# v's weight sums moved behind k's head norm on GpSimd's queue, seven gate blocks in front, v's plain products first, and another order of the projections beside the pairs

## The chip, the cores and the metric

The kernel runs on one core of a Trainium2 chip. TensorE (PE) multiplies, VectorE (DVE) and ScalarE (ACT) work on tiles of up to 128 partitions in SBUF and PSUM, GpSimd (POOL) does small vector work and issues the accumulating transfers, SyncE (SP) issues most of the others. The metric is the device time of one execution in microseconds (us). Three runs of the kernel before took 416.15, 417.72 and 417.67 us, median 417.67. The trace comes from one more, profiled execution.

## The reference

One decoder layer on x (512 tokens by 1024 features, float32) with two attention branches of 8 heads of 64 each.

```python
h = rms_norm(x, norm_w)
qa, ka, va, za, qb, kb, vb, zb, gl_a, gl_b = split(h @ w_in)      # widths 512 x 8, then 1024 x 2
oa = moba(rms_norm(qa), rms_norm(ka), va, rel_bias)               # softmax branch "a", q and k normed by head
ob = stick_breaking(qb, kb, vb)                                   # branch "b": sigmoid and a running product
ya = (oa * silu(za)) @ w_up_moba
yb = (ob * silu(zb)) @ w_up_sb
y  = sigmoid(gl_a + gb_a) * ya + sigmoid(gl_b + gb_b) * yb
out = x + y @ w_out
```

## The kernel before

**Products.** Every float32 product is made of three matmuls in fp32r: each operand is split into a high part (an ACT copy into an fp32r tile, `wh` L163, `xh`) and a low part (a DVE subtraction, `wl` L165, `xl`), and `mm3` (L202 to L206) adds high x low, low x high and high x high. A weight block is 128 x 1024 (`wr`, 512 KB). `load_w` keeps three blocks ahead in the order of the list `stream`: SP loads, ACT makes `wh`, DVE makes `wl`. A block of a projection (`chunk_ct`) is 24 matmuls of 128x512.

**Stages.** First the q projection of branch a (`qa`, 96 matmuls), then k (`ka`, 96). Both get a norm by head: ACT squares (`kasq` L323), DVE reduces (L324), POOL makes the factor of each row in three small instructions for each of four row tiles (`kast` L325 to L327), DVE multiplies (`kan` L334), transposes (`kat` L353), and the result goes through DRAM (`kadr`) and comes back turned. Meanwhile PE does the first gate projections (`gl`, the list FRONT). In this stage DVE also makes the sums of x that the next stage needs (`mix_x`, L291 to L305: four half-width additions for each of four k, and two subtractions `ml`).

**v by seven products.** The two v projections (1024 columns together) are a 2 x 2 block product done with seven products instead of eight (Strassen's scheme in Winograd's form): sums `s1` to `s4` of x, and sums T1 to T4 of the weight blocks. `sum_v` (L108) makes a weight sum by DMA: it loads one block (L117, ACT's queue) and adds the other by an accumulating transfer from POOL's queue (L120). T2 is made of T1, and T4 of T2. `product` takes two weight blocks (24 matmuls) and adds up in two PSUM banks.

**Pairs.** Then come eight pairs of heads, four of branch a and four of branch b. For each: `scores` (12 pairs of matmuls), `softmax` or `stick` on DVE and ACT, `turn` (DVE transposes, L475), `put` (SP stores the weights of the head, L482) and `get` (ACT's queue loads them turned, L489: `pta` or `ptb`). `finish` of the pair before multiplies the weights with v (`poa`, `pob`, L501, 16 matmuls) and DVE multiplies by the silu gate (L505).

**What sets the order.** Beside each pair PE gets whole blocks of other projections, written out by hand in FILLS: four words for each pair (an empty word is no block), `za`/`zb` the silu gates, `q`/`k` the operands of branch b, `g` gates, `up` the two halves of a block of the up projection (each half one PSUM bank, evacuated by DVE, L617). These take turns in two PSUM banks ("pj"), which `finish` uses too. The row of a pair so holds three or four blocks. Instructions of an engine run in the order in which the program puts them on its queue; a scheduler has settled that order when the program is built.

Of the kernel before, what the change touches and what calls it, by code (L numbers as in the profile page):

```python
# [32 lines left out]
PQ = BLK[-1] * 32  # L33
# [9 lines left out]
Y_SUMS = {0: ("T2b",), 2: ("T3a", "T3b"), 5: ("T4a", "T4b")}  # L43


FRONT = ("g:0", "g:1", "g:2", "g:3", "g:4", "g:5")
FILLS = ("za:0", "za:1", "za:2", "",
         "za:3", "g:6", "g:7", "q:0",
         "k:0", "zb:0", "q:1", "",
         "k:1", "zb:1", "q:2", "k:2",  # L50
         "zb:2", "q:3", "k:3", "",
         "zb:3", "up:0", "g:8", "up:1",
         "g:9", "up:2", "g:10", "",
         "up:3", "g:11", "g:12", "",
         "g:13", "g:14", "g:15")


@with_exitstack
def hybrid_layer(ctx: ExitStack, tc: tile.TileContext, x, xT, w, rel, out):
    nc = tc.nc  # L60
    V, A, G, T = nc.vector, nc.scalar, nc.gpsimd, nc.tensor
# [37 lines left out]
    ahead, low, sums = [], {}, {}  # L99
    turn_of = cp.tile([1, 1], F32, name="turn_of")  # L100
    WO = w.shape[0] - len(BLOCKS)
    WV, VOUT = 8, [("v", name) for name in OUT]
    stream = list(range(WV)) + list(range(16, 16 + len(FRONT))) + VOUT + list(range(16 + len(FRONT), WO)) + OUT

    def block(name, base):
        return w[base + BLOCKS.index(name)]

    def sum_v(name, part):  # L108

        with tc.issue_after(last["qa"]):  # L110
            if name == "T4":
                sums["v", "T4" + part] = t = sums["v", "T2" + part]
            else:
                t = vp.tile([P, H // 2, 2, P], F32, tag="v", name=f"v{name}{part}").rearrange("p a b d -> p (a b d)")
                sums["v", name + part] = t
                with tc.issue_after(spread_r):
                    nc.scalar.dma_start(t, block(TERMS[name][0] + part, WV))  # L117
            two = TERMS[name][1] if name != "T4" else "21"
            src = sums["v", two + part] if two[0] == "T" else block(two + part, WV)
            nc.gpsimd.dma_start(t, src, accum_op=ALU.add)  # L120
# [161 lines left out]
    def normalize(k):  # L282

        raw = xraw[k]
        V.scalar_tensor_tensor(raw, raw, nw[:, k:k + 1], R, op0=ALU.mult, op1=ALU.mult)
        A.activation(xH[k], raw, AF.Copy)
        V.tensor_tensor(xL[k], raw, xH[k].bitcast(F32), op=ALU.subtract)
# [3 lines left out]
    def mix_x(k):  # L291

        a, b = xraw[k], xraw[k + 4]
        left, right = slice(0, HS), slice(HS, S)
        V.tensor_tensor(b[:, right], a[:, right], b[:, right], op=ALU.subtract)
        V.tensor_tensor(a[:, right], a[:, left], a[:, right], op=ALU.subtract)
        V.tensor_tensor(a[:, left], b[:, right], a[:, left], op=ALU.subtract)
        V.tensor_tensor(b[:, left], b[:, left], a[:, left], op=ALU.add)
        h = tp.tile([P, 4 * PQ], F32R, tag="pt", bufs=4, name=f"mx{k}")
        for n, raw in enumerate((a, b)):  # L300
            hi, lo = h[:, n * S:(n + 1) * S], slot(f"ml{k}{n}", F32R)
            A.activation(hi, raw, AF.Copy)
            V.tensor_tensor(lo, raw, hi.bitcast(F32), op=ALU.subtract)
            for cs, name in ((left, ("S2", "S4")[n]), (right, ("S3", "S1")[n])):
                mixed[name, k] = hi[:, cs], lo[:, cs]  # L305
# [94 lines left out]
    def bring(name):  # L400
        raws[name] = fetch(flipped[name], name)

    ps_ka = section_tc(1, "ka", hooks={0: lambda: norm(ps_qa, "qa", float(HD)),
                                       1: lambda: (normalize(0), normalize(1)),
                                       2: lambda: (normalize(2), normalize(3),
                                                   [sum_v(n, h) for n in ("T1", "T2", "T3") for h in "ab"]),
                                       3: lambda: (normalize(4), normalize(5), normalize(6), normalize(7),
                                                   spread(ps_qa, "qa"))})

# [119 lines left out]

    for i, word in enumerate(FRONT):  # L530
        f_g(int(word.split(":")[1]))
        if i == 0:
            norm(ps_ka, "ka", 1.0)
            bring("qa")
        elif i == 1:
            spread(ps_ka, "ka")
            mix_x(0)
        elif i == 2:
            qa.extend(split_flipped(raws["qa"], "qa"))
            mix_x(1)  # L540
        elif i == 3:
            bring("ka")
            mix_x(2)
        elif i == 4:
            mix_x(3)

    def product(ps, a, start):
# [8 lines left out]
    def values():  # L556

        v_of = {}
        for br in "ab":
            two = [vp.tile([P, H // 2, 2, P], F32, tag="v", name=f"v{br}s{t}").rearrange("p a b d -> p (a b d)")  # L560
                   for t in range(2)]
            v_of[br] = [two[t // 2][:, t % 2 * S:(t % 2 + 1) * S] for t in range(NT)]
        a11, a12 = ([(xH[k + d][:, :HS], xL[k + d][:, :HS]) for k in range(4)] for d in (0, 4))
        a22 = [(xH[k + 4][:, HS:], xL[k + 4][:, HS:]) for k in range(4)]
        s1, s2, s3, s4 = ([mixed[f"S{n}", k] for k in range(4)] for n in (1, 2, 3, 4))
        X, Z = ([bank("s", f"v{n}{t}") for t in range(2)] for n in "xz")
        product(X, a11, True)
        for t in range(2):
            A.activation(v_of["a"][t], X[t], AF.Copy)
        product(Z, a12, True)  # L570
        for t in range(2):
            V.tensor_tensor(v_of["a"][t], Z[t], v_of["a"][t], op=ALU.add)
        product(X, s2, False)
        for t in range(2):
            A.activation(v_of["b"][t], X[t], AF.Copy, scale=-1.0)
        ka.extend(split_flipped(raws["ka"], "ka"))
        Y = [bank("s", f"vy{t}") for t in range(2)]
        product(Y, s1, True)
        for t in range(2):
            A.activation(v_of["b"][2 + t], Y[t], AF.Copy)  # L580
        for h in "ab":
            sum_v("T4", h)
        product(X, s3, False)
        for t in range(2):
            V.tensor_tensor(v_of["b"][2 + t], v_of["b"][2 + t], X[t], op=ALU.subtract)
        product(Y, s4, False)
        for t in range(2):
            V.tensor_tensor(v_of["b"][t], Y[t], v_of["b"][t], op=ALU.add)
        product(X, a22, False)
        for t in range(2):  # L590
            A.activation(v_of["a"][2 + t], X[t], AF.Copy)
        return v_of
# [268 lines left out]
```

## Time and profile before

| | us |
|---|---|
| median of three runs (416.15, 417.72, 417.67) | 417.67 |
| the profiled execution | 416.63 |
| its span in the trace | 414.8 |
| PE busy | 390.6 |
| DVE busy | 287.6 |
| ACT busy | 208.3 |
| POOL busy | 68.1 |
| granted TensorE clock, mean over the span | 0.975 |

PE is busy 94% of the span, so the time is PE's work and PE's stops. PE works without a stop through the v products, from 92.35 to 130.52 us. A view by windows gives, for a stretch of time, the busy time and the count of the instructions of each engine, then the granted TensorE clock, the busy share of the DMA engines and the GB/s. A row of the timeline gives the start, the duration, the engine, the line and the tiles, and in brackets how long the engine had been idle before it and what ended that.

### The profile page before, as it was taken

How to read it: one execution, taken by the hardware profiler on the slowest of the kernel's cores; microseconds unless marked ns; L12 is line 12 of the kernel's file. 1: busy time of each engine (PE TensorE's matmuls, PEld its weight loads, DVE VectorE, ACT ScalarE, POOL GpSimd, SP SyncE). 2: the span in 40 equal slices, each digit the busy share in tenths (PEclk: the TensorE clock that was granted, in tenths of full speed). 3: DMA queues.
4: the chain of work that ended last, by engine and by line, in shares of the span. 5: the costliest groups of instructions: out<-in, count | busy, mean ns of one | idle time of the engine just before them, and what ended most of it. 6: DMA issues, size and time to landing. Idle time of an engine off the chain costs nothing. (4 is left out here: it accounts for less than half of the span.)

```text
span 414.8 us, 5373 instructions
## 1 busy us (share of the span) xinstructions
PE 390.6 (94%) x1829; PEld 308.3 (74%) x1829; DVE 287.6 (69%) x571; ACT 208.3 (50%) x357; POOL 68.1 (16%) x110
## 2 busy tenths in 40 slices
PE   9999999399999999999799997999797999999996
PEld 5888777288888887878568775787674887888885
DVE  5645994867566888296853987748949422899963
ACT  5675452927546788365642726226352233348540
POOL 7949239101000000000000000001001000230210
PEclk9999999699999999999989997999998999999999
DMA  8958999773433486937548156886577552599935
GB/s 276 342 205 292 313 259 278 227 272 111 91 103 113 136 281 192 322 113 202 219 126 278 27 170 215 223 254 191 144 268 197 177 171 96 170 234 311 183 96 173
DMA packets 36699, 83.49 MB, mean 201 GB/s; under 512 B 4024, under 2 KB 16824, under 8 KB 36672
## 3 DMA queue, kind: packets, MB, share of 16 engines
q1 hardware_dynamic: 28112, 53.51, 39.2%
q0 software_dynamic: 4096, 13.65, 15.4%
q10 hardware_dynamic: 4464, 15.99, 11.3%
q8 instruction: 14, 0.23, 0.2%
q14 instruction: 13, 0.11, 0.1%
HBM read 65.29 MB, written 14.70 MB: 193 GB/s over the span
## 5 line engine op out<-in xcount | busy, mean ns | idle before, releaser
L165 DVE TENSOR_TENSOR wl<-wr,wh 128x1024 fp32r<-128x1024 f32 (+1 forms) x62 | 73.2, 1182 | 48.9 <-ACT wh L163 48.4
L163 ACT ACTIVATE wh<-wr 128x1024 fp32r<-128x1024 f32 (+1 forms) x62 | 63.7, 1028 | 34.8 <-PE ya L206 15.6
L205 PE MATMUL gl<-xh,wl 128*128 128x512 f32 x128 | 50.8, 397 | 6.3 <-DVE wl L165 6.3
L204 PE MATMUL gl<-xl,wh 128*128 128x512 f32 x128 | 51.1, 399 | 4.3 <-DVE gl L617 2.2
L206 PE MATMUL gl<-xh,wh 128*128 128x512 f32 x128 | 50.3, 393 | 0.0
L527 ACT ACTIVATE gl<-gl,x 128x512 f32<-128x512 f32 x16 | 11.0, 687 | 47.5 <-PE gl L206 37.7
L204 PEld LDWEIGHTS gl<-xl,wh 128*128 128x128 f32 x128 | 24.4, 191 | 13.3 <-ACT wh L163 3.6
L205 PEld LDWEIGHTS gl<-xh,wl 128*128 128x128 f32 x128 | 24.4, 191 | 11.5 <-DVE wl L165 6.6
L124 POOL COPY turn_of<-ptb 1x1 f32<-1x1 f32 x3 | 0.7, 248 | 194.0 <-DMA ptb<-pdb 194.0
L206 PEld LDWEIGHTS gl<-xh,wh 128*128 128x128 f32 x128 | 24.5, 191 | 5.1
L460 DVE TENSOR_TENSOR_SCAN sx<-om,begin 128x512 f32<-128x512 f32 (+3 forms) x32 | 24.7, 806 | 3.3 <-ACT om L456 3.3
L444 ACT ACTIVATE pa<-pa,m 128x512 f32<-128x512 f32 (+3 forms) x32 | 17.8, 558 | 10.8 <-DVE m L442 6.6
L442 DVE CUSTOM_DVE_ANT_0 pa<-sa,om 128x512 f32<-128x512 f32 (+3 forms) x32 | 15.0, 476 | 4.7 <-PE sa L432 4.7
L456 ACT ACTIVATE om<-sb 128x512 f32<-128x512 f32 (+3 forms) x32 | 14.8, 468 | 3.5 <-DVE sx L460 2.9
L475 DVE STREAM_TRANSPOSE turneda<-pa 128x256 f32<-128x256 f32 (+1 forms) x48 | 16.5, 377 | 0.1
L204 PE MATMUL zb<-xl,wh 128*128 128x512 f32 x32 | 13.4, 420 | 3.1 <-DVE kb3l L343 3.1
L204 PE MATMUL ya<-ola,wh 128*128 128x512 f32 x32 | 13.3, 416 | 3.1 <-DVE ob L505 3.1
L475 DVE STREAM_TRANSPOSE turnedb<-pb 128x256 f32<-128x256 f32 (+1 forms) x48 | 15.5, 370 | 0.0
L458 ACT ACTIVATE pb<-sb 128x512 f32<-128x512 f32 (+3 forms) x32 | 15.0, 477 | 0.0
L265 POOL TENSOR_SCALAR e_sb<-rb 8x1 f32<-8x1 f32 (+11 forms) x32 | 14.2, 474 | 1.1 <-DMA rb<-in_rel 1.1
L462 DVE TENSOR_TENSOR pb<-pb,sx 128x512 f32<-128x512 f32 (+3 forms) x32 | 14.3, 475 | 0.1
L501 PE MATMUL poa<-pta,vas 128*64 128x128 f32 (+3 forms) x64 | 11.6, 496 | 2.5 <-DMA pta<-pda 2.5
(359 smaller groups left out, 1013.5 us busy)
## 6 DMA issues: line engine op xcount, KB each, us to landing
wr<-in_w SPq DMA_DIRECT2D x58, 512.0 KB, 5.3
pda<-turneda SPq DMA_DIRECT2D x32, 160.0 KB, 2.6
pta<-pda ACTq DMA_DIRECT2D x8, 640.0 KB, 5.4
pdb<-turnedb SPq DMA_DIRECT2D x32, 160.0 KB, 2.7
ptb<-pdb ACTq DMA_DIRECT2D x8, 640.0 KB, 4.3
xn<-in_x SPq DMA_DIRECT2D x8, 256.0 KB, 5.9
om<-e_dr SPq DMA_DIRECT2D x8, 256.0 KB, 5.9
xr<-in_xT SPq DMA_DIRECT2D x7, 256.0 KB, 5.7
```

The source lines that it names most:

```text
L163: A.activation(hi[:, a:b], raw[:, a:b], AF.Copy)
L165: low[c] = V.tensor_tensor(lo[:, a:b], raw[:, a:b], hi[:, a:b].bitcast(F32), op=ALU.subtract).ins
L204: T.matmul(ps, aH, bL, start=start, stop=False, skip_group_check=on)
L205: T.matmul(ps, aL, bH, start=False, stop=False, skip_group_check=on)
L206: T.matmul(ps, aH, bH, start=False, stop=stop, skip_group_check=on)
L442: V.tensor_tensor_reduce(p, sc[i], bias[:, S - n:], scale=1.0, scalar=3e38, op0=ALU.add, op1=ALU.min, accum_out=m[:, 0:1])
L444: A.activation(p, p, AF.Exp, bias=m[:, 0:1], scale=-1.0, accum_out=m[:, 1:2])
L456: A.activation(om[:, e - 1 - n:e - 1], z, AF.Sigmoid, scale=-1.0)
L458: A.activation(p, z, AF.Sigmoid)
L460: V.tensor_tensor_scan(sx[:, n - 1::-1] if n == S else sx[:, :n][:, ::-1], om[:, e - n:][:, ::-1], begin[:, S - n:][:, ::-1], 0.0, op0=ALU ...
L462: V.tensor_tensor(p, p, sx[:, :n], op=ALU.mult)
L475: V.transpose(turned[:, :, at:at + (n - 1) * step + 1:step, :].rearrange("p q j r -> p j q r"), rows[i][:, j * P:(j + n) * P].rearrange("p ...
```

## The change

- `sum_v` for T1, T2 and T3 is no longer called while k is projected, but beside the gates 3, 4 and 5 of the front, each after the last instruction of k's head norm on POOL (`last["ka"]` in place of `last["qa"]`). The six loads move from ACT's queue to POOL's.
- FRONT has seven gates instead of six; `mix_x(k)` goes one gate later. The low parts `ml` get other buffers.
- The order of v's products was a11, a12, s2 (T2), s1 (T1), s3 (T3), s4 (block 22), a22 (T4). It is now a11, a12, s4, s2, s1, s3, a22. The result of s4 is kept in a new tile `top` until s2 and s1 are there. a22 now follows directly on s3, in the same two banks.
- FILLS: the rows of the four a pairs held 3, 4, 3, 4 blocks and now hold 3, 3, 3, 3; those of the b pairs held 3, 4, 3, 3 (with g:13 and g:14 behind the last) and now hold 4, 4, 4, 4. g:15 stays last.

The instructions that compute stay the same in number on PE. In what follows a row is the line, the instruction and the tiles it writes and reads; lines of the new kernel are three to thirteen higher than before.

On POOL, at k's head norm (`kast`), before:

```order
L327 TENSOR_SCALAR qast<-qast,r 128x8 [waits Pool_49]
L120 DMA vT1a<-in_w 128x1024 [waits DMAHW1_49]
L120 DMA vT1b<-in_w 128x1024 [waits DMAHW3_49]
L120 DMA vT2a<-vT1a 128x1024 [waits DMAHW4_49,DMASW2_49]
L120 DMA vT2b<-vT1b 128x1024 [waits DMAHW6_49,DMASW3_49]
L120 DMA vT3a<-in_w 128x1024 [waits DMAHW7_49]
L120 DMA vT3b<-in_w 128x1024 [waits DMAHW0_49]
L325 TENSOR_SCALAR kast<-kast,r2ka 128x8 [waits DVE_49]
L326 TENSOR_TENSOR kast<-kast,half 128x8 [waits Pool_49]
L327 TENSOR_SCALAR kast<-kast,r 128x8 [waits Pool_49]
```

and now, from the last of the twelve `kast` instructions on:

```order
L331 TENSOR_SCALAR kast<-kast,r 128x8 [waits Pool_49]
L116 DMA vT1a<-in_w 128x1024
L116 DMA vT1b<-in_w 128x1024
L116 DMA vT2a<-in_w 128x1024
L119 DMA vT1a<-in_w 128x1024 [waits DMASW2_49]
L119 DMA vT1b<-in_w 128x1024 [waits DMASW3_49]
L116 DMA vT2b<-in_w 128x1024
L119 DMA vT2a<-vT1a 128x1024 [waits DMASW5_49,DMASW4_49]
L116 DMA vT3a<-in_w 128x1024 [waits DMAHW6_49,DMAHW5_49,DMAHW7_49,DMAHW4_49,DMASW1_49]
L119 DMA vT2b<-vT1b 128x1024 [waits DMASW7_49,DMASW6_49]
L116 DMA vT3b<-in_w 128x1024 [waits DMAHW4_49,DMAHW5_49,DMAHW1_49,DMAHW0_49]
L119 DMA vT3a<-in_w 128x1024 [waits DMASW1_49]
```

Six transfers stood between q's norm and k's; now none does, and twelve stand behind k's.

On ACT, at the second `get` of the softmax pairs. Before, in the third pair (the tile numbers tell buffers apart):

```order
L489 DMA pta_1794<-pda_1754 128x1280
L342 ACTIVATE qb1h<-qb_1875 128x512
L163 ACTIVATE wh_1988<-wr_1986 128x1024
L444 ACT_TABLE_LOAD
L444 ACTIVATE pa_1950,m_1951<-pa_1950,m_1951 128x512
L444 ACTIVATE pa_1956,m_1957<-pa_1956,m_1957 128x384
L489 DMA pta_1867<-pda_1828 128x1280
```

and now, in the second pair:

```order
L492 DMA pta_1559<-pda_1520 128x1280
L346 ACTIVATE kb1h<-kb_1656 128x512
L162 ACTIVATE wh_1769<-wr_1767 128x1024
L447 ACT_TABLE_LOAD
L447 ACTIVATE pa_1731,m_1732<-pa_1731,m_1732 128x512
L447 ACTIVATE pa_1737,m_1738<-pa_1737,m_1738 128x384
L492 DMA pta_1648<-pda_1593 128x1280
```

The same sequence now stands in the second pair, and again in the third and the fourth: the second head's load comes behind the evacuation of the row's last block and behind two exponentials of the next pair.

On DVE, in the row of the second b pair (zb:2, up:0, g:9, up:1), at the end of its second head, now:

```order
L478 STREAM_TRANSPOSE turnedb_2539<-pb_2522 128x4x32
L478 STREAM_TRANSPOSE turnedb_2539<-pb_2528 128x2x4x32
L517 TENSOR_TENSOR zb_2510<-zb_2485,zb_2510 128x512
L478 STREAM_TRANSPOSE turnedb_2539<-pb_2534 128x4x32
L164 TENSOR_TENSOR wl_2554<-wr_2551,wh_2553 128x1024
L630 TENSOR_TENSOR gl_610<-ya_2557,gl_610 128x512
L630 TENSOR_TENSOR gl_676<-ya_2571,gl_676 128x512
```

L517 is the instruction that frees the bank of zb:2 (`zb_2485`); it stands near the end of the transposes, and the second half of up:0 (`ya_2571`) takes that bank. The row of the third b pair (zb:3, up:2, g:10, up:3) has the same order.

```diff
-FRONT = ("g:0", "g:1", "g:2", "g:3", "g:4", "g:5")
-FILLS = ("za:0", "za:1", "za:2", "",
-         "za:3", "g:6", "g:7", "q:0",
-         "k:0", "zb:0", "q:1", "",
-         "k:1", "zb:1", "q:2", "k:2",
-         "zb:2", "q:3", "k:3", "",
-         "zb:3", "up:0", "g:8", "up:1",
-         "g:9", "up:2", "g:10", "",
-         "up:3", "g:11", "g:12", "",
-         "g:13", "g:14", "g:15")
+FRONT = ("g:0", "g:1", "g:2", "g:3", "g:4", "g:5", "g:6")
+FILLS = ("za:0", "q:0", "k:0", "",
+         "za:1", "q:1", "k:1", "",
+         "za:2", "q:2", "k:2", "",
+         "za:3", "q:3", "k:3", "",
+         "zb:0", "zb:1", "g:7", "g:8",
+         "zb:2", "up:0", "g:9", "up:1",
+         "zb:3", "up:2", "g:10", "up:3",
+         "g:11", "g:12", "g:13", "g:14",
+         "", "", "g:15")
...
-    WV, VOUT = 8, [("v", name) for name in OUT]
+    WV, VOUT = 8, [("v", b + h) for b in ("11", "21", "22", "T2", "T1", "T3", "T4") for h in "ab"]
...
-        with tc.issue_after(last["qa"]):
+        with tc.issue_after(last["ka"]):
...
-                with tc.issue_after(spread_r):
-                    nc.scalar.dma_start(t, block(TERMS[name][0] + part, WV))
+                nc.gpsimd.dma_start(t, block(TERMS[name][0] + part, WV))
...
-                                       2: lambda: (normalize(2), normalize(3),
-                                                   [sum_v(n, h) for n in ("T1", "T2", "T3") for h in "ab"]),
+                                       2: lambda: (normalize(2), normalize(3)),
...
         elif i == 1:
             spread(ps_ka, "ka")
-            mix_x(0)
         elif i == 2:
             qa.extend(split_flipped(raws["qa"], "qa"))
-            mix_x(1)
+            mix_x(0)
         elif i == 3:
             bring("ka")
+            for half in "ab":
+                sum_v("T1", half)
+            mix_x(1)
+        elif i == 4:
+            for half in "ab":
+                sum_v("T2", half)
             mix_x(2)
-        elif i == 4:
+        elif i == 5:
+            for half in "ab":
+                sum_v("T3", half)
             mix_x(3)
...
+        product(Y, s4, True)
+        top = [slot(f"vb{t}") for t in range(2)]
+        for t in range(2):
+            A.activation(top[t], Y[t], AF.Copy)
         product(X, s2, False)
         for t in range(2):
-            A.activation(v_of["b"][t], X[t], AF.Copy, scale=-1.0)
+            V.tensor_tensor(top[t], top[t], X[t], op=ALU.subtract)
...
+        for t in range(2):
+            V.tensor_tensor(v_of["b"][t], Y[t], top[t], op=ALU.add)
         product(X, s3, False)
...
-        product(Y, s4, False)
-        for t in range(2):
-            V.tensor_tensor(v_of["b"][t], Y[t], v_of["b"][t], op=ALU.add)
         product(X, a22, False)
```

More of the change, by code (lines that the diff above doesn't have):

```diff
@@ L299, in mix_x @@
         h = tp.tile([P, 4 * PQ], F32R, tag="pt", bufs=4, name=f"mx{k}")
+        if k < 2:
+            l = tp.tile([P, 4 * PQ], F32R, tag="turned", bufs=2, name=f"ml{k}")
+            l = [l[:, n * S:(n + 1) * S] for n in range(2)]
+        else:
+            l = [tp.tile([P, S], F32R, tag=("p3", "sx")[n], bufs=2, name=f"ml{k}{n}") for n in range(2)]
         for n, raw in enumerate((a, b)):
-            hi, lo = h[:, n * S:(n + 1) * S], slot(f"ml{k}{n}", F32R)
+            hi, lo = h[:, n * S:(n + 1) * S], l[n]
             A.activation(hi, raw, AF.Copy)
@@ L565, in values @@
         s1, s2, s3, s4 = ([mixed[f"S{n}", k] for k in range(4)] for n in (1, 2, 3, 4))
-        X, Z = ([bank("s", f"v{n}{t}") for t in range(2)] for n in "xz")
+        X, Z, Y = ([bank("s", f"v{n}{t}") for t in range(2)] for n in "xzy")
         product(X, a11, True)
@@ L572, in values @@
             V.tensor_tensor(v_of["a"][t], Z[t], v_of["a"][t], op=ALU.add)
+        product(Y, s4, True)
+        top = [slot(f"vb{t}") for t in range(2)]
+        for t in range(2):
+            A.activation(top[t], Y[t], AF.Copy)
         product(X, s2, False)
         for t in range(2):
-            A.activation(v_of["b"][t], X[t], AF.Copy, scale=-1.0)
+            V.tensor_tensor(top[t], top[t], X[t], op=ALU.subtract)
         ka.extend(split_flipped(raws["ka"], "ka"))
-        Y = [bank("s", f"vy{t}") for t in range(2)]
+        for h in "ab":
+            sum_v("T4", h)
+        Y = [bank("s", f"vw{t}") for t in range(2)]
         product(Y, s1, True)
@@ L580, in values @@
             A.activation(v_of["b"][2 + t], Y[t], AF.Copy)
-        for h in "ab":
-            sum_v("T4", h)
+        for t in range(2):
+            V.tensor_tensor(v_of["b"][t], Y[t], top[t], op=ALU.add)
         product(X, s3, False)
```

## The prediction

> **What bounds the kernel now.** I read the page first, then the waits of PE, then a view by windows cut at the starts of the stages, and last the timelines around each stop.
>
> ```profile
> span 414.8 us, 5373 instructions
> PE 390.6 (94%) x1829; PEld 308.3 (74%) x1829; DVE 287.6 (69%) x571; ACT 208.3 (50%) x357; POOL 68.1 (16%) x110
> ...
> PE gl L205 <- DVE wl L165: 6.3, 1, 6.3
> PE zb L204 <- DVE kb3l L343: 3.1, 1, 3.1
> PE ya L204 <- DVE ob L505: 3.1, 1, 3.1
> PE poa L501 <- DMA pta<-pda: 2.5, 1, 2.5
> ...
> PE gl L204 <- DVE gl L617: 2.2, 1, 2.2
> ```
>
> PE is the bound: it works 94% of the span, and the change leaves its instructions alone. So only PE's stops, and the clock granted after them, can move the time. The windows price both. Behind the time range stand its length, PE's busy time, and near the end the granted clock:
>
> ```profile
> 48.86:92.35 43.49, 35.10 (x145) 27.88 (x144) 33.17 (x63) 22.00 (x33) 15.16 (x16) 0.92 0.93 266
> 92.35:130.52 38.17, 38.17 (x169) 31.34 (x167) 23.26 (x24) 21.37 (x26) 1.83 (x2) 1.00 0.36 99
> 149.12:175.69 26.57, 26.57 (x138) 20.73 (x137) 17.81 (x53) 16.94 (x29) 0.00 (x0) 1.00 0.81 260
> 175.69:196.62 20.93, 20.93 (x113) 16.28 (x112) 16.27 (x52) 12.56 (x25) 0.00 (x0) 1.00 0.56 164
> 196.62:227.80 31.18, 28.70 (x137) 21.70 (x136) 18.53 (x54) 14.46 (x27) 0.00 (x0) 0.95 0.63 208
> 227.80:249.16 21.36, 21.25 (x115) 16.22 (x114) 18.91 (x36) 10.65 (x23) 0.00 (x0) 1.00 0.36 100
> 249.16:282.06 32.90, 29.82 (x137) 22.94 (x136) 21.53 (x39) 11.94 (x24) 1.63 (x3) 0.90 0.72 224
> 282.06:305.47 23.41, 21.23 (x114) 16.22 (x113) 18.91 (x36) 9.86 (x21) 1.58 (x3) 1.00 0.72 212
> 305.47:351.16 45.69, 42.24 (x201) 32.27 (x201) 23.39 (x40) 15.90 (x29) 1.81 (x3) 0.96 0.55 168
> ```
>
> The first row is the six front gates, the second v's seven products, the others run from one pair's first score to the next one's: pair 1 (counted from 0) to pair 6, and last pair 7 with everything up to the up projection of branch b. v's 38.17 us for seven groups of 24 matmuls, without a stop, make 5.45 us a block. Pairs 1 and 2 ran without a stop: a row with four blocks takes 26.57 us, one with three 20.93. Against these the losses are: front 43.49 - 6 x 5.45 = 10.8; pair 3 (four blocks) 31.18 - 26.57 = 4.6; pair 4 (three) 0.4; pair 5 (four) 6.3; pair 6 (three) 2.5. Pair 7 holds 12 score pairs, six blocks and two `pob`: 20.93 + 3 x 5.45 + 2.3 (row below) = 39.6, so it lost 6.1. Sum 30.7 us. The waits name only half of it. The rest is slow clock behind them: pair 6's wait of 2.2 cost 2.5 at clock 1.00, while pair 3's 2.5 cost 4.6 at 0.95 and pair 5's 3.1 cost 6.3 at 0.90.
>
> **Part 1, the front.** Whom does the 6.3 us stop wait for?
>
> ```profile
> 53.38 0.87 POOL L120 DMA_DIRECT2D vT2a<-vT1a  x1 [9.02 <-DMA vT1a<-in_w]
> ...
> 61.71 2.80 POOL L325 TENSOR_SCALAR kast<-kast,r2ka 128x8 f32<-128x8 f32 x1
> ...
> 66.46 0.31 POOL L327 TENSOR_SCALAR kast<-kast,r 128x8 f32<-128x8 f32 x1
> ...
> 74.02 0.31 POOL L327 TENSOR_SCALAR kast<-kast,r 128x8 f32<-128x8 f32 x1
> ...
> 55.73 1.28 DVE L324 TENSOR_REDUCE kast<-kasq 128x8 f32<-128x512 f32 x2
> ...
> 64.40 0.43 DVE L298 TENSOR_TENSOR xr<-xr,xr 128x256 f32<-128x256 f32 x1
> ...
> 74.97 2.72 DVE L353 STREAM_TRANSPOSE kat<-kan 128x256 f32<-128x256 f32 x8
> ...
> 78.79 2.35 DVE L165 TENSOR_TENSOR wl<-wr,wh 128x1024 fp32r<-128x1024 f32 x2
> ```
>
> DVE's `wl` at 78.79 stands behind `kat`, which needs `kast` from POOL, and POOL began `kast` at 61.71 because six accumulating transfers stood ahead, one waiting 9.02 us for another. The reduces that `kast` needs began at 55.73. The change puts all transfers behind `kast`: it starts at about 56.4, and at the pitch of (74.02 - 66.46) / 3 = 2.52 us, plus the 2.80 of its first instruction, ends at 66.5 instead of 74.3. DVE then isn't free at once: the additions of `mix_x`, which ended at 64.8, now come a gate later and with five `ml` still ahead of `kan`. I put `kan` at 70 to 72.6, `kat` (2.72) until 75.4, and one subtraction and the `wl` of gate 5 until about 77.2. PE, without a stop, wants gate 5 at 48.86 + 0.5 + 5 x 5.45 = 76.6. Loss in front 1.0 us (0.5 for an early wait that stays, 0.5 here), against 10.8. Bounds: none of it, or the stop moved to gate 5 at half its size with slow clock, 6 to 7.
>
> **Part 2, the sums now late.** Twelve software transfers queue behind `kast` from 66.5 on, the waits of the accumulations block POOL, and nothing but sums stands behind them. How long they take:
>
> ```profile
> L117 ACTq DMA_DIRECT2D vT1a<-in_w x1: 340/340/340, 34.9 to 34.9; - x1
> ...
> DMA to landing us min/median/max: 3.4/6.0/15.3
> ...
> DMA to landing us min/median/max: 5.3/9.2/13.3
> ```
>
> The second row is of the loads, the third of the accumulations. T2 takes a load and two accumulations in series: by medians 6.0 + 2 x 9.2 = 24.4, landing at 91; by the largest 15.3 + 2 x 13.3 = 41.9, at 108. v starts one gate later but 9.8 us sooner, at 92.35 - 9.8 + 5.45 = 88.0; three plain products come first, so PE wants T2 at 104.4, less two splits at about 102. Cost 0, cover 11 us; at the far end 6 us and slow clock. The first row of windows has the DMA engines 0.93 busy, so their bytes move, they don't vanish.
>
> The product order costs PE nothing else: a22 starts in the bank whose DVE subtraction is due while PE still does 6 matmuls (1.4 us) in the other one. ACT's and DVE's extra `top` pieces lie in a stage with DVE busy 23.26 of 38.17. Without that cover it would cost those 1.4 us at most; I take 0.
>
> **Part 3, softmax rows of three blocks.** Pair 3's stop:
>
> ```profile
> 196.73 0.60 ACT L342 ACTIVATE qb1h<-qb 128x512 fp32r<-128x512 f32 x1 [3.89 <-PE qb L206]
> ...
> 200.55 0.33 ACTq L489 DMA_DIRECT2D pta<-pda  x1
> ...
> 205.68 4.06 PE L501 MATMUL poa<-pta,vas 128*64 128x128 f32 x14 [2.48 <-DMA pta<-pda]
> ...
> 311.08 2.37 PE L501 MATMUL pob<-ptb,vbs 128*64 128x128 f32 x14 [0.39 <-DMA ptb<-pdb]
> ```
>
> After a row of three blocks the second head's load stands on ACT behind the row's last evacuation and two exponentials of the next pair: issued 3.9 us after that pair's first score (196.62), landed at 205.68, while PE has only 17 matmuls for cover. After the row of four in pair 1 there was no stop. Now pairs 1, 2 and 3 all have three blocks and that order on ACT, so pairs 2, 3 and 4 should each stop as pair 3 did: 4.6 + 4.6, and 4.0 in pair 4, where six sigmoids stand ahead of the load in place of a table load and two exponentials. Sum 13.2 against 4.6. Bounds: 0 (the load lands in time) to 3 x 6.3, pair 5's loss.
>
> **Part 4, the b rows.** Four blocks each, so the loads have their cover, and the stops of pairs 5 and 7 on `kb3l` and `ob` go: k:3 now ends a softmax row, and DVE evacuates it ahead of the next pair's scans; behind the last `ob` stand gates, which ACT evacuates. But in pairs 5 and 6 the second half of an `up` block takes the bank of the zb block before it, and DVE frees that near the end of its second head.
>
> ```profile
> 284.40 2.07 DVE L460 TENSOR_TENSOR_SCAN sx<-om,begin 128x512 f32<-128x512 f32 x2
> ...
> 296.56 1.48 DVE L475 STREAM_TRANSPOSE turnedb<-pb 128x256 f32<-128x256 f32 x5
> ...
> 297.96 1.18 DVE L165 TENSOR_TENSOR wl<-wr,wh 128x1024 fp32r<-128x1024 f32 x1
> ```
>
> In pair 6 DVE's transposes ended 15.9 us after the first score (282.06). PE comes there after scores (2.1), `pob` (2.3), one block and half of the next: 2.1 + 2.3 + 5.45 + 2.7 = 12.5. Wait 3.4 us; behind a wait of 3.1 to 3.5 pairs 5 and 7 lost another 3.2 and 2.6, so 2.6 to 3.2 more. I take 3.4 + 2.6 = 6.0 each (pair 7 ran the same `ya` matmuls behind its wait), 12.0 in all, where before pairs 5 and 6 lost 8.8. Bounds: 0 (DVE earlier) to 2 x 6.6. Pair 7 keeps about 0.8 for its last load, of 6.1.
>
> **The sum.** Losses after: 1.0 + 0 + 13.2 + 12.0 + 0.8 = 27.0, before 30.7: 3.7 us less. The profiled execution took 416.63 (its span 414.8), so 412.9; it stands 1.0 below the median of the runs, within their spread (416.15 to 417.72). I predict 413.
>
> A page speaks to the slow clock. The Trainium skill, "TensorE: Matmul & The Clock Gate", Part 1, says that the clock halves only after an idle window of about 3.4 us. By that rule the waits of 2.5 to 3.4 us cost no clock, and the time is rival D's. The trace disagrees: after 2.48 us of waiting 14 `poa` took 4.06 us instead of 2.37.
>
> **Rivals.**
>
> - A (0.50): as summed, 413, its own range 407 to 417.
> - B (0.15), the other side: the second `get` in pairs 2 to 4 lands later than the 5.1 us of pair 3. For it: pair 1's window has the DMA engines 0.81 busy, and three rows in a run would meet that load. Against it: those rows' transfers are the same in number as before. Break-even is a loss of 30.7 - 1.0 - 12.0 - 0.8 = 16.9 in the three, 5.6 each, so a landing 1.0 us later; at 2.1 us later it is 6.7 each, 20.1 in all, the loss 33.9 and the time 419.8.
> - C (0.07): T2 lands at 108, by the largest rows. PE waits 6 us in v and loses 2.5 more to slow clock: 421.4. Against it: those rows fell in a stretch where sums, turns and weights all met.
> - D (0.18): the short waits cost no clock, or not every row stops. Pair 6 is the example: 2.2 us and clock 1.00. Then the three loads cost 2.5 each and the banks 3.4 each: 14.3 + 1.8 = 16.1, 14.6 less than before: 402.
> - E (0.10): the front gains half. `wl` of gate 5 stands behind `kan`; if DVE reaches `kan` 3 us later than I put it, PE stops 3.5 and loses 2.4 more, 5.4 above the 0.5 of the sum: 418.3, no change. Against it: between the last addition (64.8) and `kat` (75.0) DVE had only the four `kan` to do.
>
> **How the numbers follow.** This kernel's runs spread over 0.4%, so 0.5% (2.1 us) is what can be told from none: faster is below 415.6, slower above 419.8. Faster: 0.40 of A and all of D, 0.58. Same: 0.10 of A, 0.08 of E, half of B, 0.25. Slower: the rest of B, C and E, 0.17. Range 402 to 420: it holds A, E, half of D and two thirds of B, and leaves out C and the far ends of B and D, some 0.2.
>
> **What would show it.** Front: POOL's first `kast` at 56 to 57, no wait of PE on `wl` over 1 us before 88, v's first product at 87 to 89. Sums: no wait of PE on a split in v. Softmax rows: three waits `poa` on `pta`, 2 to 3 us each, with a clock below 1 behind them. Stick rows: two waits of `ya` on DVE's gate product L517, about 3.4 us each. It is wrong if the front still stops, if the `poa` waits are missing or twice as long, or if PE stops in v.

## The result: slower by 1%, and the profile after

The changed kernel takes 420.52 us (median of 11 runs), the kernel before 416.76 (11 runs): a ratio of 1.0108, 95% interval 1.0068 to 1.0148. I had predicted 413, with a range of 402 to 420. The profiled execution of the changed kernel took 419.05 us, its span is 417.3, against 416.63 and 414.8 before. The ratios here and below leave out executions more than 1.5% above the fastest of their kernel, so they are not quite the quotients of the medians.

The page, and the waits of PE in the changed kernel (us in total, times, longest). The weight splits and `mm3` stand one line earlier than before (`wh` L162, `wl` L164, `mm3` L203 to L205), the lines of the pairs three later:

```profile
PE 390.7 (94%) x1829; PEld 308.5 (74%) x1829; DVE 288.2 (69%) x573; ACT 203.3 (49%) x353; POOL 69.1 (17%) x116
...
PE vx L203 <- DVE wl L164: 7.9, 1, 7.9
PE ya L203 <- DVE zb L517: 6.2, 2, 3.6
PE poa L504 <- DMA pta<-pda: 4.3, 2, 2.7
PE poa L504 <- DVE m L445: 1.7, 1, 1.7
PE vy L203 <- DVE wl L164: 1.0, 1, 1.0
```

The stop in front is gone, and a longer one, 7.9 us, stands at v's first product, where there was none. The windows, cut as in the prediction (seven gates; v but its last product; pairs 2 to 6; pair 7 up to the up projection of branch b):

```profile
48.88:87.78 38.90, 38.74 (x170) 31.38 (x168) 32.72 (x63) 20.74 (x31) 17.90 (x20) 1.00 0.77 224
87.78:132.80 45.02, 36.07 (x148) 28.42 (x146) 22.48 (x25) 20.89 (x27) 4.87 (x6) 0.89 0.73 204
...
177.95:201.13 23.18, 21.56 (x114) 16.60 (x113) 16.64 (x52) 12.92 (x25) 0.00 (x0) 1.00 0.74 224
201.13:225.94 24.81, 23.16 (x113) 17.74 (x112) 16.58 (x52) 12.92 (x25) 0.00 (x0) 0.93 0.58 174
225.94:255.65 29.71, 27.01 (x138) 21.11 (x137) 20.31 (x37) 12.39 (x25) 0.18 (x1) 1.00 0.62 193
255.65:285.90 30.25, 26.72 (x137) 20.71 (x136) 20.83 (x38) 11.99 (x24) 2.18 (x4) 1.00 0.68 194
285.90:318.89 32.99, 29.43 (x138) 22.77 (x138) 21.51 (x39) 11.42 (x23) 1.59 (x3) 0.90 0.59 176
318.89:353.75 34.86, 34.86 (x178) 26.70 (x177) 21.63 (x38) 14.35 (x27) 0.87 (x1) 1.00 0.59 183
```

Against the same full paces (5.45 us a block, 20.93 a row of three, 26.57 a row of four) the losses are: front 38.90 - 7 x 5.45 = 0.7; v 45.02 - 6 x 5.45 - 0.4 (two score matmuls) = 11.9; pairs 2 to 6 2.3, 3.9, 3.1, 3.7 and 6.4; pair 7 34.86 - 34.1 = 0.7. That is 32.7 in place of 30.7, and the span is 2.5 longer.

What did PE wait for in v? Timeline rows of ACT and PE:

```profile
79.94 15.03 ACTq L368 DMA_DIRECT2D kaT<-kadr  x4
95.02 1.27 ACT L530 ACTIVATE gl<-gl,x 128x512 f32<-128x512 f32 x2 [15.18 <-DMA wr<-in_w]
96.23 1.06 ACT L162 ACTIVATE wh<-wr 128x1024 fp32r<-128x1024 f32 x1
...
98.60 0.80 PE L203 MATMUL vx<-wl,xh 128*128 128x512 f32 x1 [7.94 <-DVE wl L164]
```

ACT stood for 15 us at the four loads that bring k back turned (`kaT`), and the high part of v's second weight block stands behind them. But the block itself was no sooner there. SP issued it at 80.97, right behind k's eight stores, and the issues in the window 80.9 to 81 us give its time to landing:

```profile
wr<-in_w SPq DMA_DIRECT2D x1, 512.0 KB, 15.2
```

So it landed at 96.2, and `wh` began at 96.23, when ACT too had just done its two `gl`. ACT's stand and the block's landing ended together. The transfers of that stretch say why both were late. First the changed kernel from 70 to 116 us (queue 0 is POOL's; the last number of the other rows is the median from issue to landing), then the kernel before from 70 to 100 us:

```profile
q0 software_dynamic: 1728, 6.29, 53.8%
...
wr<-in_w SPq DMA_DIRECT2D x8, 512.0 KB, 8.2
...
kadr<-kat SPq DMA_DIRECT2D x8, 128.0 KB, 7.6
```

```profile
q0 software_dynamic: 55, 0.16, 2.7%
...
wr<-in_w SPq DMA_DIRECT2D x6, 512.0 KB, 3.7
kadr<-kat SPq DMA_DIRECT2D x8, 128.0 KB, 2.3
```

The packets of the twelve sum transfers took 53.8% of the time of the 16 engines. Beside them k's stores landed three times as late, and the plain weight blocks twice as late by the median; the three that SP issued next behind k's stores took 15.0 to 17.3 us, before 4.3 to 6.8.

### The profile page after: what moved, and what is told of

The parts are those of the page before. It is cut to its first block, busy times and chain, and to the rows that moved or that the text cites. A ratio compares the mean times of both kernels' runs of the same rounds, so it can differ in the third digit from the quotient of the medians.

```text
span 417.3 us, 5376 instructions
## 1 busy us (share of the span) xinstructions
PE 390.7 (94%) x1829; PEld 308.5 (74%) x1829; DVE 288.2 (69%) x573; ACT 203.3 (49%) x353; POOL 69.1 (17%) x116
## 4 chain that ended last, share of the span: by engine, by line
PE 55%; DVE 22%; DMA 13%; ACT 6%; issue 3%; SPq 1%; POOL 0%; DVEq 0%; ACTq 0%
DMA wr<-in_w 6%; PE gl L203 4%; PE gl L204 4%; PE gl L205 4%; DVE wl L164 4%; DVE sx L463 3%; DMA pta<-pda 3%; ACT wh L162 2%; PE poa L504 2%; PE yb L205 2%; PE yb L204 2%; PE yb L203 2%; PE ya L203 2%; PE ox L204 2%; PE ox L205 2%
## 5 line engine op out<-in xcount | busy, mean ns | idle before, releaser
L164 DVE TENSOR_TENSOR wl<-wr,wh 128x1024 fp32r<-128x1024 f32 (+1 forms) x62 | 73.2, 1182 | 70.2 <-ACT wh L162 70.0
L162 ACT ACTIVATE wh<-wr 128x1024 fp32r<-128x1024 f32 (+1 forms) x62 | 63.7, 1028 | 50.8 <-DMA wr<-in_w 21.9
L203 PE MATMUL gl<-xl,wh 128*128 128x512 f32 x128 | 50.5, 395 | 0.0
L205 PE MATMUL gl<-xh,wh 128*128 128x512 f32 x128 | 49.9, 390 | 0.0
L203 PEld LDWEIGHTS gl<-xl,wh 128*128 128x128 f32 x128 | 24.2, 189 | 7.2 <-issue 1.0
L205 PEld LDWEIGHTS gl<-xh,wh 128*128 128x128 f32 x128 | 24.1, 189 | 5.1
L203 PE MATMUL ya<-ola,wh 128*128 128x512 f32 x32 | 13.7, 428 | 6.2 <-DVE zb L517 6.2
L504 PE MATMUL poa<-pta,vas 128*64 128x128 f32 (+3 forms) x64 | 10.7, 441 | 6.0 <-DMA pta<-pda 4.3
L203 PE MATMUL vx<-wl,xh 128*128 128x512 f32 x16 | 7.5, 467 | 7.9 <-DVE wl L164 7.9
```

The source lines that it names most:

```text
L162: A.activation(hi[:, a:b], raw[:, a:b], AF.Copy)
L164: low[c] = V.tensor_tensor(lo[:, a:b], raw[:, a:b], hi[:, a:b].bitcast(F32), op=ALU.subtract).ins
L203: T.matmul(ps, aH, bL, start=start, stop=False, skip_group_check=on)
L205: T.matmul(ps, aH, bH, start=False, stop=stop, skip_group_check=on)
L504: T.matmul(po[o, :].rearrange("p (a n) -> p a n", a=4)[:, :, j * 32:], vv[j][:, c:c + HD], src, start=j == NT - 1, stop=j == 0, skip_group ...
```

## The experiments

In the table, A is the time from the first gate to the second pair's first score, less 5.45 us for each gate (PE without a stop: 56.8 before, by the windows 92.35 to 130.52 and 130.52 to 149.12); B the time from there to the up projection of branch b, less 5.45 us for the two kernels with one more block there. Both are of the profiled execution, and behind B every kernel runs 63.5 to 63.7 us to the end of its span. The ratio is to the kernel before, from runs on the same chip.

| kernel | median us | ratio (95%) | A | B |
|---|---|---|---|---|
| before | 416.76 | 1 | 67.6 | 196.6 |
| changed | 420.52 | 1.0108 (1.0068 to 1.0148) | 69.8 | 196.9 |
| loads on ACT | 424.85 | 1.0207 (1.0149 to 1.0265) | 71.4 | 198.2 |
| kaT's loads later | 416.56 | 0.9978 (0.9933 to 1.0024) | 66.5 | 198.6 |
| no accumulations | 412.35 | 0.9840 (0.9794 to 0.9886) | 59.9 | - |
| accumulations as plain copies | 414.80 | 0.9956 (0.9912 to 1.0000) | 64.9 | 198.4 |
| old rows | 421.35 | 1.0112 (1.0069 to 1.0155) | 73.6 | 195.5 |
| before with the changed rows | 420.05 | 1.0070 (1.0023 to 1.0118) | 66.9 | 200.2 |
| other rows | 411.68 | 0.9884 (0.9833 to 0.9935) | 71.3 | 187.9 |
| split sums | 417.97 | 1.0006 (0.9959 to 1.0054) | 64.8 | 200.4 |
| split sums, other rows, kaT later | 405.36 | 0.9742 (0.9665 to 0.9818) | 64.9 | 187.8 |
| the same, T3 later | 402.37 | 0.9672 (0.9615 to 0.9729) | 61.9 | 186.7 |
| the same, q's loads later | 400.29 | 0.9636 (0.9563 to 0.9709) | 59.4 | 186.9 |
| that front with the changed rows | 410.95 | 0.9897 (0.9832 to 0.9963) | 59.3 | 195.2 |

B differs by up to 5 us between kernels with the same rows (195.2 to 200.4), so 2 or 3 us there tell nothing by themselves. Of the kernel without accumulations only the front is read.

### Whose stop is it in v?

Two theories. T: the sums' traffic makes everything else land late. O: the order on ACT, with `kaT` ahead of v's splits, does it whatever the traffic. Five runs.

**The six loads back on ACT's queue, early.** Only the six accumulations stay behind `kast`.

```diff
+    def load_v(name, part):
+        ...
+        with tc.issue_after(spread_r):
+            nc.scalar.dma_start(t, block(TERMS[name][0] + part, WV))
...
-                nc.gpsimd.dma_start(t, block(TERMS[name][0] + part, WV))
...
+                                                   [load_v(n, h) for n in ("T1", "T2", "T3") for h in "ab"]),
```

> The changed kernel, with the six loads of T1, T2, T3 back on ACT's queue at the place they had before (34 to 41 us); the six accumulations stay behind kast. Theory T (traffic): in the changed kernel twelve software transfers fill the DMA engines from 70 to 116 us, kadr's stores land up to 14.9 us late, and ACT, which holds kaT's loads behind them, makes v's second weight split 8 us late. Half of the transfers gone from that stretch: PE's stop at v's first product falls from 7.9 to under 3 us, the loss in v from 12.1 to 2 to 5 us, time 411 to 415. Rival O (order): the stop comes from kaT's loads standing ahead of v's splits on ACT, whatever the traffic: stop stays over 6 us, time 419 to 422.

Measured: 424.85 us, worse than the change. From its transfers in the window 70 to 116 us and its timeline:

```profile
q0 software_dynamic: 864, 3.15, 38.5%
...
kadr<-kat SPq DMA_DIRECT2D x8, 128.0 KB, 13.0
...
99.83 0.79 PE L207 MATMUL vx<-wl,xh 128*128 128x512 f32 x1 [7.36 <-DVE wl L168]
```

The stop stayed, against what I expected of T. But neither is this O: with half the transfers gone, k's stores landed later still (13.0 us), and v's second block, issued behind them at 84.84, landed only at 97.2. What differs is that three accumulations were now issued back to back just ahead of the stores (69.9 to 71.2 us), not one by one behind their loads; that this is the reason I conclude from the order, no run isolates it. The number of transfers was the wrong measure.

**kaT's loads later on ACT.**

```diff
         elif i == 3:
-            bring("ka")
...
         product(Z, a12, True)
         for t in range(2):
             V.tensor_tensor(v_of["a"][t], Z[t], v_of["a"][t], op=ALU.add)
+        bring("ka")
```

> The changed kernel, with only the four loads of kaT issued later on ACT's queue, behind v's splits for a11 and a12. Rival O (ACT's order alone): the stop of 7.9 us in v's first product goes, none comes after it, loss in v under 3 us, time 409 to 413. Theory T (traffic): the stop at the first product goes too, since ACT is free, but the v weights themselves land late (8 us median in that stretch): stops of 2 to 6 us in the products that follow, time 413 to 418. Neither right if the weight of the second half block itself lands only at 95: the stop stays, 420.

Measured: 416.56 us, and the stop at the same place is 4.89 us:

```profile
93.91 1.06 ACT L162 ACTIVATE wh<-wr 128x1024 fp32r<-128x1024 f32 x1 [9.96 <-DMA wr<-in_w]
...
96.28 0.80 PE L203 MATMUL vx<-wl,xh 128*128 128x512 f32 x1 [4.89 <-DVE wl L164]
```

ACT is free now, and it waits 10 us for the weight block itself, which SP issued at 79.91, right behind k's eight stores, and which landed 13.9 us later. So there were two ways to the same stop, and freeing ACT left the other. The 3 us that came off it are the block's: it was issued 1.1 us sooner and landed 1.3 us faster than in the changed kernel, perhaps because `kaT`'s loads were no longer under way beside it. O alone is out.

**No accumulations, and accumulations as plain copies.** In both the weight sums are left out, so v is another. The first drops the six accumulating transfers and keeps the loads; the second keeps all twelve in their order but lets the six copy.

```diff
-            nc.gpsimd.dma_start(t, src, accum_op=ALU.add)
+            if name == "T4":
+                nc.gpsimd.dma_start(t, src, accum_op=ALU.add)
```

> The changed kernel without the six accumulating transfers of T1, T2 and T3 (the weight sums are left out, so v is another); their six loads stay on POOL's queue. Theory T: with half the software bytes kadr lands in 2 to 5 us, the stop in v goes to 0 to 2 us, time 408 to 411. Rival O: the stop stays over 5 us, time 418 to 421. Beside the run with the loads on ACT it tells loads from accumulations.

```diff
-            nc.gpsimd.dma_start(t, src, accum_op=ALU.add)
+            nc.gpsimd.dma_start(t, src, **({"accum_op": ALU.add} if name == "T4" else {}))
```

> The changed kernel with the same twelve transfers on POOL's queue, but the six accumulating ones of T1, T2 and T3 as plain copies into the same tiles (the weight sums are left out, so v is another). The bytes moved and the order stay. If it is the accumulation that makes the engines late (in the trace with the loads on ACT's queue six of them took 38.5% of 46 us, near 3 us of all engines each, twice a plain load): the stop in v's first product falls from 7.9 to 2 to 4 us, time 413 to 417. If twelve software transfers of any kind do it: stop 6 to 9 us, time 419 to 422.

Measured: 412.35 and 414.80 us. The first product of v in the one, and the share of POOL's queue and the first product in the other:

```profile
92.81 0.50 PE L204 MATMUL vx<-wl,xh 128*128 128x512 f32 x1 [1.40 <-DVE wl L165]
```

```profile
q0 software_dynamic: 1993, 7.31, 51.4%
...
95.89 0.50 PE L203 MATMUL vx<-wl,xh 128*128 128x512 f32 x1 [3.77 <-DVE wl L164]
```

Without the accumulations the stop is 1.40 us; as plain copies, with the same bytes and the same order, 3.77; accumulating, 7.94. T holds, in a sharper form: the accumulations weigh most. And in all five kernels `wh` begins 0.05 to 0.25 us behind the landing of v's second block, so in none could the stop have ended sooner. From its issue behind k's stores the block took 15.2 us in the changed kernel, 12.4 with the loads on ACT, 13.9 with `kaT` later, 11.1 with plain copies and 4.2 without the accumulations. The landing of k's stores is the poorer measure: without the accumulations they still took 9.6 us, where I expected 2 to 5.

The rows give the weight of an accumulation. In the run with early loads six of them took 38.5% of 46 us, 2.95 us of all 16 engines each. With plain copies twelve of these and two accumulations (T4) took 51.4%, 23.6 us; less 2 x 2.95 that is 1.5 us for a copy. The shares of the changed kernel agree: 53.8% of 46 us is 24.7, less 6 x 1.5 leaves 2.6 for an accumulation. And in the kernel before the two of T4 ran almost alone, from 100 to 116 us:

```profile
q0 software_dynamic: 288, 1.05, 36.4%
```

That is 5.8 us for two, 2.9 each, with almost nothing beside them.

**The old rows with the changed front.** FRONT and FILLS as before, all else as changed.

```diff
-FRONT = ("g:0", "g:1", "g:2", "g:3", "g:4", "g:5", "g:6")
+FRONT = ("g:0", "g:1", "g:2", "g:3", "g:4", "g:5")
... and FILLS as before
```

> The changed kernel with FRONT and FILLS as before (six gates, the old rows), the sums, the product order and the buffers as changed. If the rows' new order is worth what the trace after shows (pairs 1 to 7 lost 20.3 us, before 19.9), the time stays within 2 us of the changed kernel's: 419 to 422. If the new rows gain (as the prediction had it not, but three waits of 1.6 to 2.7 us with no slow clock suggest), it is over 422. One gate less in front leaves the sums 5.45 us less before v wants T2: a second stop in v of 0 to 5 us would be seen there.

Measured: 421.35 us. One gate less in front did not come back as time: PE was at v 4.3 us sooner, and then stopped longer, 13.11 us ahead of the second product, which began at 102.2 us where the changed kernel began it at 103.7.

```profile
102.21 0.79 PE L203 MATMUL vz<-wl,xh 128*128 128x512 f32 x1 [13.11 <-DVE wl L164]
```

The block that `wh` waited for landed at 99.8 here. So up to about 100 us the transfers set the pace, and blocks put in front of v or taken away only move the waiting. The pairs, with the old rows, lost no more than the changed ones (B 195.5).

### What are the rows worth?

**The changed rows on the kernel before.**

```diff
+FRONT = ("g:0", "g:1", "g:2", "g:3", "g:4", "g:5", "g:6")
+FILLS as changed
```

> The kernel before with FRONT and FILLS of the changed kernel (seven gates, the new rows), and nothing else. By the traces the rows as changed lose 20.3 us in pairs 1 to 7, the old ones 19.9: time 416 to 419, no change from before. If the prediction's prices for the rows (25.2 after, of 19.9) held: 420 to 423.

Measured: 420.05 us, a ratio of 1.0070 (1.0023 to 1.0118): slower than the kernel before by 2.9 us, B 200.2 against 196.6. The trace's "no change" was too good and my first price too high. The stops are those of the changed kernel, and two thirds of the front's old one:

```profile
PE ya L204 <- DVE zb L514: 6.2, 2, 3.6
PE poa L501 <- DMA pta<-pda: 6.0, 3, 2.7
PE gl L205 <- DVE wl L165: 4.0, 1, 4.0
```

**Other rows.** Pairs 1 to 3 get a fourth block, and in the b rows a gate stands ahead of zb and up.

```diff
-         "za:1", "q:1", "k:1", "",
-         "za:2", "q:2", "k:2", "",
-         "za:3", "q:3", "k:3", "",
-         "zb:0", "zb:1", "g:7", "g:8",
-         "zb:2", "up:0", "g:9", "up:1",
-         "zb:3", "up:2", "g:10", "up:3",
-         "g:11", "g:12", "g:13", "g:14",
+         "za:1", "q:1", "k:1", "g:7",
+         "za:2", "q:2", "k:2", "g:8",
+         "za:3", "q:3", "k:3", "g:9",
+         "g:10", "zb:0", "up:0", "",
+         "g:11", "zb:1", "up:1", "",
+         "g:12", "zb:2", "up:2", "",
+         "g:13", "g:14", "zb:3", "up:3",
```

> The changed kernel with other FILLS: the rows of a pairs 1 to 3 get a fourth block, a gate (g:7 to g:9), and in the b rows a gate stands ahead of zb and up (g, zb, up), so that up's second half no longer follows zb in its bank by half a block; 3 blocks in the first three b rows, 4 in the last. Theory R (rows): a stop of poa on pta comes from rows of three blocks, one of ya on L517 from the bank. Both go: pairs 2 to 6 lost 19.3 us in the changed kernel and lose 3 to 9 here; new short stops of pob on ptb, 0 to 3 us each, in the three-block b rows. Time 408 to 415. Rival: what is freed in one row comes back in the next (DVE and ACT set the pace of a pair, about 25 us, whatever the blocks): losses stay over 15, time 417 to 421. The stop in v stays 5 to 9 us by both.

Measured: 411.68 us, B 187.9. PE's waits:

```profile
PE vx L203 <- DVE wl L164: 9.5, 1, 9.5
PE pob L504 <- DMA ptb<-pdb: 2.5, 2, 2.1
```

No `poa` waits for its load, and no `ya` for zb's bank. The run changes both kinds of row at once, but each stop stood in rows of its own kind, and both came with the changed rows on the kernel before: rows of three softmax blocks make the one, half a block between zb and up's second half the other. The loads still take 3.8 to 7.3 us (3.8 to 8.8 in the changed kernel), but PE comes to them later: in pair 2 it began `poa` 4.5 us after the first head's load had landed. The rival, that freed time comes back in the next row, is out: 9 us less in B, and as much in the time. v's stop stayed.

### A front that keeps its gain

**Split sums.** The loads early on ACT; the accumulations of T1 and T3 ahead of `kast`, as before; only T2's, which had to wait for T1's, behind it.

```diff
-        with tc.issue_after(last["ka"]):
+        with tc.issue_after(last["ka" if name in ("T2", "T4") else "qa"]):
...
+                                                   [load_v(n, h) for n in ("T1", "T3", "T2") for h in "ab"],
+                                                   [sum_v(n, h) for n in ("T1", "T3") for h in "ab"]),
```

> The changed kernel with the six loads on ACT as before, the four accumulations of T1 and T3 ahead of kast as before, and only T2's two, which waited for T1's, behind kast. Theory T, as the runs without accumulations (stop 1.4 us) and with the loads away (7.4 us) narrowed it: the accumulations fill the DMA engines. With two instead of six behind kast the stop in v's first product is 0 to 2 us. POOL has no transfer to wait for but T3's load, so kast starts at 56 to 60 and the front loses 1 to 4 us. Time 408 to 413. Rival: the accumulations at 42 to 60 make q's way through DRAM late (ACT stood 5.1 us behind qadr before), the front loses 5 to 8 us: 413 to 418.

Measured: 417.97 us. v has no stop, but the fifth gate (g:4) has:

```profile
77.40 0.50 PE L208 MATMUL gl<-xh,wl 128*128 128x512 f32 x1 [4.16 <-DVE wl L168]
...
50.51 13.12 SPq L363 DMA_DIRECT2D qadr<-qat  x8
63.76 6.42 SPq L157 DMA_DIRECT2D wr<-in_w  x3
...
65.13 1.06 ACT L166 ACTIVATE wh<-wr 128x1024 fp32r<-128x1024 f32 x1 [4.82 <-DMA qadr<-qat]
```

The rival was right here. The four accumulations from 43 to 60 us do to q what the twelve did to k: SP takes 13 us to issue q's stores (about 3 of them waiting for DVE's last two transposes), the next weights stand behind them, and ACT stands behind q's loads. DVE then has the splits and sums of x late, and `wl` of g:4 runs at 76.15, behind `kan` and `kat`.

**With the other rows and kaT's loads later** (both edits as above):

> The last two edits together, with kaT's loads issued behind v's first two products. If front and rows are independent, the losses add up: front and v 2 to 5 us, pairs 5 to 11 us, in place of 33: time 396 to 408. If not: over 410, and the place of the new stop tells which of them depends on the other.

Measured: 405.36 us, A 64.9 and B 187.8: each as in the run with that edit alone, so front and rows are independent, as expected.

**T3's accumulations later**, behind the last x sum that DVE makes:

```diff
-                                                   [sum_v(n, h) for n in ("T1", "T3") for h in "ab"]),
+                                                   [sum_v("T1", h) for h in "ab"]),
...
         product(X, a11, True)
+        for h in "ab":
+            sum_v("T3", h)
...
-        with tc.issue_after(last["ka" if name in ("T2", "T4") else "qa"]):
+        with tc.issue_after(last["qa"] if name == "T1" else G.tensor_copy(turn_of, mixed["S2", 3][1][:1, :1].bitcast(F32)).ins if name == "T3" else last["ka"]):
```

> The version with split sums and new rows (405.36), with T3's two accumulations issued only when the last x sum is made (about 82 us) in place of 44 to 54. Left at 43 to 60 are T1's two. In that version q's stores took 12.5 us to issue, ACT stood 4.2 us behind them and PE stopped 4.2 us at gate 5 (front loss 7.9). Theory T: with half of the early accumulations q's stores land in time; front loss 1 to 4 us, v 0 to 2 us, time 399 to 404. Rival: four accumulations from 70 to 95 make v's weights late again, stop in v 2 to 5 us: 404 to 409.

Measured: 402.37 us, A 61.9. The stop at g:4 is 1.82 us, and v runs without one.

**q's loads later too**, behind g:5, their splits in v:

```diff
         if i == 0:
             norm(ps_ka, "ka", 1.0)
-            bring("qa")
...
         elif i == 5:
+            bring("qa")
             mix_x(3)
...
+        qa.extend(split_flipped(raws["qa"], "qa"))
         bring("ka")
```

> As the run with T3's accumulations late, and q's loads out of DRAM and their splits issued later too (behind gate 5, the splits behind v's second product), so that ACT can't stand behind q's stores while it owes PE a weight split. If ACT's stand was what was left of the front's stop: loss in front 0 to 2 us, time 398 to 403. If it was the weights themselves (SP's next loads stand behind q's stores): the same as the run without this edit.

Measured: 400.29 us, a ratio of 0.9636 (0.9563 to 0.9709) to the kernel before: the best of all. Its page, PE's waits, and the windows of the front and of v:

```profile
span 397.4 us, 5371 instructions
PE 386.7 (97%) x1829; PEld 304.8 (77%) x1829; DVE 289.9 (73%) x573; ACT 202.1 (51%) x353; POOL 67.7 (17%) x112
...
PE gl L207 <- DVE gl L634: 1.4, 1, 1.4
PE pob L510 <- DMA ptb<-pdb: 1.1, 2, 0.8
...
49.14:89.54 40.40, 38.75 (x170) 31.30 (x169) 31.93 (x61) 18.95 (x27) 14.71 (x18) 1.00 0.84 227
89.54:128.43 38.89, 38.89 (x172) 31.59 (x170) 27.25 (x31) 25.78 (x34) 1.73 (x2) 1.00 0.57 177
```

The same sums are made with the same transfers, but only two accumulations now stand ahead of q's stores (issued at 43 us), two ahead of k's (69 us), and two come in v (82 us); and ACT, which waits for q's and k's ways through DRAM, owes PE nothing in the meantime. The runs of this kernel and of the one before it overlap, so the last step is better read from A, 2.5 us less. The stop at g:4 is 0.8 us in place of 1.8, and the clock over the front 1.00 in place of 0.96. That it was ACT's stand behind q's loads, as I expected, isn't shown: in both kernels `wl` of g:4 stands on DVE behind `kat`, which waits for POOL's last `kast`.

**That front with the changed rows**, to see the front alone:

> The best version so far (400.29) with the rows of the changed kernel in place of the new ones: the changed kernel with its front mended alone. If front and rows add up, the front is worth 12.8 - 3 = 10 us against the changed kernel and the rows 8 to 10 more: 408 to 412 here. If the mended front only passes its stops on to the pairs: over 415.

Measured: 410.95 us, A 59.3 and B 195.2. The front is worth about 10 us to the changed kernel, the other rows about 10 more.

## Why the prediction was wrong

**Part 1, the front, held.** `kast` began when its reduces were there, DVE was at `kan` and `kat` within half a microsecond of the forecast, and PE waited 0.2 us for g:5 where I had 0.5. Loss 0.7, predicted 1.0. Some of that was luck. Four times 2.52 us from 56.4 make 66.5; with the 2.80 that I named beside them, `kast` ends at 69.3, and it did end at 69.9. That cost nothing because DVE was at the sums of x until 70.1 anyway.

```profile
56.45 0.27 POOL L329 TENSOR_SCALAR kast<-kast,r2ka 128x8 f32<-128x8 f32 x1 [16.58 <-DVE kast L328]
...
69.83 0.69 POOL L116 DMA_DIRECT2D vT1a<-in_w  x1
...
70.07 2.48 DVE L338 TENSOR_TENSOR kan<-ka,kast 128x512 f32<-128x512 f32 x4
72.46 2.72 DVE L357 STREAM_TRANSPOSE kat<-kan 128x256 f32<-128x256 f32 x8
...
76.95 0.50 PE L204 MATMUL gl<-xh,wl 128*128 128x512 f32 x1 [0.16 <-DVE wl L164]
```

**Part 2 failed: "Cost 0, cover 11 us".** I asked only when the sums themselves would land, and that part held: T2 landed at 99.3, later than the 91 of the medians but ahead of the 102 at which its splits were due, and no split of T2 made PE wait. "Nothing but sums stands behind them" is true of POOL's queue and false of the engines. The step I left out is what twelve transfers, the six accumulations above all, do to others in the same 40 us: k's stores, k's loads, and v's plain weights, whose second block landed 15.2 us after its issue and stopped PE for 7.9 us. I even wrote that the bytes "move, they don't vanish", and gave that sentence no price. Measured, it is the 11.9 us that v lost (waits of 7.9 and 1.0, and a clock of 0.89 over the window), all of the front's gain and more. The rows of the kernel before had it: with the sums at 40 to 70 us and the engines at 0.98 to 1.07, q's stores took 6.5 us to land and k's, after the sums, 2.3. Rival C had the right place and nearly the right time (421.4) by the wrong transfer, T2 in place of the plain blocks, and too small a chance.

**Part 3 came near in number, but its mechanism held in one row of three.** Pairs 2, 3 and 4 stopped at `poa` for 1.6, 1.7 and 2.7 us, and lost 2.3 + 3.9 + 3.1 = 9.3; I had 13.2. The matmuls of `poa` alternate between the two heads, so the first two rows of a pair need only the first head's load, the other fourteen both:

```profile
173.66 0.33 ACTq L492 DMA_DIRECT2D pta<-pda  x1
...
181.71 0.43 PE L504 MATMUL poa<-pta,vas 128*64 128x128 f32 x2 [1.62 <-DMA pta<-pda]
...
204.92 0.40 PE L504 MATMUL poa<-pta,vas 128*64 128x128 f32 x2 [1.65 <-DVE m L445]
...
234.99 2.37 PE L504 MATMUL poa<-pta,vas 128*64 128x128 f32 x14 [2.70 <-DMA pta<-pda]
```

Only pair 4 stopped as I had it, at the second head's load (issued at 230.16, landed 4.8 us later). In pair 2 PE stopped at the first head's: issued at 173.66, it landed 8.0 us later, at 181.7. In pair 3 it stopped at the same place; the profile names a DVE instruction there, but the first head's load, issued at 195.94, landed at 204.7 too, after 8.8 us. In both rows the second head's load then came in time. That three stops came out near 2 us each was in part luck. The run with four blocks in those rows took all three away. What was over-priced is the slow clock: it followed the 1.7 us of pair 3 (clock 0.93) but not the 2.7 of pair 4 (1.00).

**Part 4 was right.** Two waits of `ya` for L517, 2.7 and 3.6 us (3.4 predicted), with losses of 3.7 and 6.4, predicted 6.0 each. Moving a gate ahead of zb took them away. **Pair 7** lost 0.7, predicted 0.8.

**The sum.** 27.0 predicted, 32.7 measured: the missing term is +11.9, and the pairs were over-priced by 5.9. So the sign hung on one term. The rows alone are a small loss (1.0070 on the kernel before, 2.9 us, where my terms for them make 26.0 against 19.9), the sums' move a gain in front that is given back in v.

## What to carry to other kernels

A transfer that is moved off a queue it blocked is still in the engines' way: list what else must land in the stretch it is moved to, and which engine stands behind each of those. When an engine waits for a transfer on its own queue, ask what it owes to others meanwhile; issuing such loads later took 4 us off one kernel here, 2.5 us off the front of another, and nothing off the front of a third. But ask too whether what it owes could have been done: in the changed kernel the weight block landed no sooner than ACT was free. Blocks that hide a latency should be counted by row: a row of four hid a load here that a row of three did not.

## What the hardware showed that I had not expected

By the time of its packets, an accumulating transfer held the 16 DMA engines for 2.6 to 2.95 us per 512 KB (2.9 with almost nothing beside it), a plain copy from the same queue for about 1.5. By the Trainium skill, "DMA: Bandwidth & Descriptors", section "Issuing engines are not separate DMA queues", transfers of all issuing engines run on the same 16 engines and interleave; the traces agree, with k's stores at 2.3 us without the sums and 7.6 to 13.0 beside them.

SP's issue itself slowed: k's eight stores of 128 KB took 4.0 us to issue in the kernel before, 6.9 in the changed kernel, and 12.7 behind three accumulations issued back to back (loads on ACT). There DVE had all of `kat` ready by 73.3 us, and the sixth store alone took 5.5 us, from 74.84. The weight loads stand behind the stores on SP's queue.

The clock's drop did not follow the length of the wait: behind 1.65 us in one row the 128x512 matmuls took 0.63 us each, behind 2.70 in the next 0.39, behind 3.56 0.63 again. The Trainium skill, "TensorE: Matmul & The Clock Gate", Part 1, calls the window that is watched free-running, which fits that scatter. Its idle time of about 3.4 us doesn't fit a drop behind 1.65. What decides it is left open.
